# Earlier query weights on GpSimd, and two steps exchanged on VectorE, in a hybrid decoder step

## The chip, the cores and the metric

The kernel runs on one core of a Trainium2 chip. The metric is the device time in microseconds (us) of one execution; several executions are timed and the median is taken. The engines are TensorE (PE in the profile, with PEld for the loads of its weights), VectorE (DVE), ScalarE (ACT), GpSimd (POOL) and SyncE (SP, which here issues DMAs).

## The reference, cut to what matters

One inference step of one decoder layer on 560 tokens: 16 meta tokens and 512 prompt tokens as one sequence, and 8 running samples of 4 new tokens with states of their own. All data are 32-bit floats.

```python
def trunk(x, W, states):
    x = x + 0.5 * swiglu(rmsnorm(x, g_ff1), ...)     # 1024 -> 2816 -> 1024
    mix, new_st = mixer(rmsnorm(x, g_mix), W, l, st)
    x = x + mix
    x = x + 0.5 * swiglu(rmsnorm(x, g_ff2), ...)
    return rmsnorm(x, g_final), states

def mlstm_chunk(q, k, v, ig, logf, C0, n0, m0):      # 4 heads of 128, in the mixer
    b = jnp.cumsum(logf, axis=-1)
    D = jnp.where(causal, b[..., :, None] - b[..., None, :] + ig[..., None, :], -jnp.inf)
    inter = b + m0[..., None]
    m = jnp.maximum(jnp.max(D, axis=-1), inter)
    w_intra = jnp.exp(D - m[..., None])
    w_inter = jnp.exp(inter - m)
    s = jnp.einsum('bhtd,bhsd->bhts', q, k) * w_intra
    num = jnp.einsum('bhts,bhse->bhte', s, v) + w_inter[..., None] * jnp.einsum('bhed,bhtd->bhte', C0, q)
    den = jnp.sum(s, axis=-1) + w_inter * jnp.einsum('bhd,bhtd->bht', n0, q)
    h = num / jnp.maximum(jnp.abs(den), jnp.exp(-m))[..., None]
    ...                                               # w_state, decay from the last token
    C = decay[..., None, None] * C0 + jnp.einsum('bhs,bhse,bhsd->bhed', w_state, v, k)
    n = decay[..., None] * n0 + jnp.einsum('bhs,bhsd->bhd', w_state, k)
    return h, (C, n, m_last)
```

The mixer has 4 such heads beside 4 tiles of 128 channels of a gated linear recurrence (RG-LRU: a short convolution, two gates from small matrices, a scan over tokens). Both halves go through one output projection. The reference takes the prompt in chunks; the kernel takes all 528 prompt tokens at once, which is the same function. For the samples the state `C0` and `n0` of each sample enter, weighted by `w_inter`.

## The kernel before, in words

**Layout.** Tokens lie along the free dimension (560 columns; `TQ` = 544 without the 16 meta tokens), channels on the 128 partitions. Every matmul of large matrices is split: each factor is a rounded high part and a low rest (`whi`/`wlo`, `xh`/`xl`, `zh`/`zl`), and three products of parts are added. ACT makes the high part with a copy, DVE the low part with a subtraction.

**Stages.** The first feed-forward block, the mixer, the output projection, the second feed-forward block and the last norm follow one another. The change is in the mixer, which takes about 430 to 570 us of the span.

**Order.** In the mixer nothing is scheduled by a planner. `PLAN` is a table of step names; a loop calls them in that order under a manual schedule, so each engine gets its instructions in the order in which the steps issue them. A name is a step and a head or channel tile: `n1` is `do_n(1)`. Each engine works through its own list in order and waits by semaphores; SP issues the DMAs in the same order.

The steps that the change and the prediction touch:

- `v`, `k`, `q`, `x`, `y`, `o`: PE products of the input projection (L296), 8 row tiles of weights each, for one tile of 128 output channels; `ev`, `ek`, `eq`, `eo`: DVE takes the result out of the accumulator with the norm's factor (L991), giving `vT`, `kT`, `qT`, `og`.
- `L(h)`: DMAs of a head: `Ab`, `Eb` (stabilisers in a row, for all partitions), `Wb` (`w_inter` of the 32 sample tokens, for all partitions), `c0` (the states, 8 samples of 128 x 128; the profile calls it `c`).
- `am`: POOL adds the causal masks to `Ab`. `w`: ACT takes exponentials, giving the weights `W` (1376 columns: five key tiles against the queries they reach, the last 32 columns the samples). `s`: PE makes the scores `pA`, `pB`. `m`: DVE multiplies `W` by the scores (L1458).
- `sd`: POOL adds `W` over key tiles into `D` (L1464 to L1468), so that one sum over partitions is left for the denominator. `hd`: `D` is split into `zh` (ACT, L1320) and `zl` (DVE, L1321).
- `qw`: POOL makes the decayed queries of the samples: `qw` = q times `Wb`, `qn` = `qw` times n0, and then adds the samples' own weights to `qn`.
- `n`: PE's phase for numerator and denominator of a head: `state(b)` (L1489) is sample b's state matrix against its four columns of `qw`, `keys(i)` (L1493) is a tile of values against `W`, `den(i)` (L1497) sums `zh` and `zl` over partitions, L1508 is the samples' own values, L1512 the sum of `qn` over partitions.
- `cn`, `cm`, `f`, `cf`: the head's norm. ACT takes squares of `pn` into `sq` and `dd`; `cm` splits the squares (`sqh` by ACT, L1531; `sql` by DVE, L1532) and takes a maximum into `dd` (DVE, L1534); `f` sums them on PE into `pv` (L1541); `cf` adds `pv` to `dd` (DVE, L1548) and takes the root.
- `cw`, `p`, `cp`: the new state. POOL decays `c` (L1568), PE makes the outer products `px` (L1559), DVE adds them to `c` (L1582); then SP issues the DMA of `c` to `out_o_cs`, and POOL makes the new n (L1587, L1588).
- `a`, `b`: the two gates of a channel tile on PE (`prg`, L1191). `cd`: DVE's scan (L1243 to L1246). `ln`, `lr`: DVE sums the recurrence's squares (`lacc`, L1259), PE sums them over partitions (`pl`, L1265), ACT takes the root (`rl`, L1272), DVE refines it (L331).
- `tv`, `tk`: PE transposes v and k (L1354 to L1356) after POOL has copied the sample columns three times (`t`, L1351).

**Accumulators.** Products, gates, transposes, `pn`, `pv` and `px` all come from one ring of three PSUM tiles, and `pden`, `py` and a few others from a ring of two:

```python
psm = ctx.enter_context(tc.tile_pool(name="psm", bufs=3, space=PSUM))
psa = ctx.enter_context(tc.tile_pool(name="psa", bufs=2, space=PSUM))
def mm_tile(name="ps"):
    return psm.tile([P, 2, 512], F32, tag="mm", name=name)
```

A tile that PE wants to write must have been read by whoever took the third one before. `qw`, `qn`, `Wb` and `c0` have two buffers each; other intermediate rows come from a pool of 23.

Of the kernel before, what the change touches and what calls it, by code (L numbers as in the profile page):

```python
# [8 lines left out]
ALU = mybir.AluOpType  # L9
# [27 lines left out]
k0 gc  # L37
q0 ek0 gd
k1 eq0 gf ge L0 ex0 cx0 tv0 gp ek1 hq0 hk0 gq hx0 gh
x1 am0 hk1 ex1 cv0  # L40
q1 a0 eq1 w0 b0 ta0 s0 m0 cx1 tk0 tb0 ck0 ca0
v1 sd0 ev1 hq1 L1 hx1 cb0 hd0 qw0 vm0 n0 cw0 a1 cc0 sk0 b1 cd0 cn0 ta1 cm0 tb1
k2 ca1 cb1 ek2 ci1 tv1 am1
x2 f0 cv1 p0 ex2 cf0 tk1 ck1 cp0 cj1 cx2
q2 L2 s1 w1 m1 sd1 eq2 hx2 hq2
v2 ev2 cd1 hd1 a2 ta2 ca2 b2 cb2 vm1 sk1 qw1 tb2 n1 cw1 cc2 cn1 hk2 am2 ce0
x3 cm1 ex3 f1 cf1 ce1
k3 w2 cl1 tv2 cx3
q3 cv2 ek3 hx3 eq3 p1 s2 tk2 cp1 cd2 ck2
v3 qw2 m2 vm2 L3 a3 sd2 hd2 ev3 n2 cw2 ta3 ca3 b3 hk3 cb3 cn2 tv3 tb3 cc3 sk2 am3 cd3  # L50
o0 p2 hq3 cv3 ce2 ce3 eo0 cl2 cl3 cm2 w3 cp2
y0 qw3 to0 ln lr ey0 gy0
o1 eo1 mo0 s3 my0 m3 f2 sd3
y1 tk3 hd3 cf2 to1 ey1 gy1 ck3 so0 mo1 n3 cw3 sk3 cn3 cm3
y2 ey2 so1 f3
# [73 lines left out]
WO = (0, 512, 912, 1184, 1328, 1344)  # L129
# [10 lines left out]
def hymba_step(ctx, tc, xT, wgu1, wdn1, win, wout, wgu2, wdn2, consts, small, c0t, wrg,  # L140
# [610 lines left out]
    kv = spill.tile([LATER, 2, P, 516], F32, name="kv")  # L751
    kv4 = spill.tile([LATER, C16, 257], F32, name="kv4")
    mixer(tc, dict(locals()))


# [133 lines left out]
def mixer(ctx, tc, e):  # L889
    nc = tc.nc  # L890
    act, dve, pool, pe = nc.scalar, nc.vector, nc.gpsimd, nc.tensor
    C, X, sm, om, osm, one_m = e["C"], e["X"], e["sm"], e["om"], e["osm"], e["one_m"]
    nm, n2 = e["nm"], e["n2"]
# [7 lines left out]
    def slot(name="slot", dtype=F32):  # L901
        return mp.tile([P, 592], dtype, tag="s", name=name, bufs=SLOTS)
# [7 lines left out]
    def blk4(ap):  # L910
        return ap.rearrange("p (b j) -> p b j", j=4)
# [392 lines left out]
    D = [{} for _ in range(H)]  # L1304
# [155 lines left out]
    @step  # L1460
    def do_sd(h):
        W = D[h]["W"]
        S = D[h]["S"] = slot("D")
        pool.tensor_copy(S[:, 0:112], W[:, 0:112])  # L1464
        pool.tensor_tensor(S[:, 112:512], W[:, 112:512], W[:, 512:912], op=ALU.add)
        pool.tensor_tensor(S[:, 240:512], S[:, 240:512], W[:, 912:1184], op=ALU.add)
        pool.tensor_tensor(S[:, 368:512], S[:, 368:512], W[:, 1184:1328], op=ALU.add)
        pool.tensor_tensor(S[:16, 496:512], S[:16, 496:512], W[:16, 1328:1344], op=ALU.add)  # L1468

    @step  # L1470
    def do_qw(h):
        d = D[h]
        qw = d["qw"] = mp.tile([P, NB, 4], F32, tag="qw", name="qw", bufs=2)
        qn = d["qn"] = mp.tile([P, NB, 4], F32, tag="qn", name="qn", bufs=2)
        pool.tensor_tensor(qw, blk4(d["q"][:, 512:TQ]), d["Wb"], op=ALU.mult)
        n0 = d["n0"] = C[:, N0 + 8 * h:N0 + 8 * h + 8]
        pool.tensor_tensor(qn, qw, n0.unsqueeze(2).to_broadcast([P, NB, 4]), op=ALU.mult)
        qs = qn.rearrange("p b j -> p (b j)")[:32]
        pool.tensor_tensor(qs, qs, d["W"][:32, WO[5]:WO[5] + 32], op=ALU.add)

    @step
    def do_n(h):
        d = D[h]
        W, V = d["W"], d["V"]
        pn, pd = ps["n", h] = mm_tile("pn"), aux_tile("pden")

        def state(*bs):
            for b in bs:
                pe.matmul(pn[:, 1, 4 * b:4 * b + 4], d["c0"][:, b, :], d["qw"][:, b, :], start=b == 0, stop=False)  # L1489

        def keys(i):
            a = T0[i] - C16
            pe.matmul(pn[:, 0, a:512], V[:KROWS[i], i, :P], W[:KROWS[i], WO[i]:WO[i] + 512 - a],  # L1493
                      start=i == 0, stop=i == 4)

        def den(i):
            pe.matmul(pd, ones_r[1], d["Ss"][i], start=i == 0, stop=i == 1)  # L1497


        state(0, 1)  # L1500
        keys(0)
        state(2, 3)
        keys(1)
        state(4, 5)
        den(0)
        state(6, 7)
        keys(2)
        pe.matmul(pn[:, 1, 0:32], d["V5"], W[:32, WO[5]:WO[5] + 32], start=False, stop=True)  # L1508
        keys(3)
        den(1)  # L1510
        keys(4)
        pe.matmul(pn[:, 1, 64:96], one_m[1], d["qn"].rearrange("p b j -> p (b j)"), start=True, stop=True)  # L1512


# [211 lines left out]
```

## Time and profile before

| | |
|---|---|
| median of 3 runs | 1022.17 us (1020.84 to 1023.37) |
| profiled execution, its own time | 1023.64 us |
| its span, first to last instruction | 1021.9 us |
| mean granted TensorE clock | 0.993 |
| HBM read, written | 95.20 MB, 6.33 MB (99 GB/s over the span) |

Engines' busy shares, the chain that ended last, the waits and the rows around the change stand in the prediction. In such rows `L1489` is a line of the kernel as printed above, `out<-in` the program's names, and a bracket tells how long the engine had been idle and which instruction the profile puts down for its release. The granted clock is 1 where TensorE runs at full speed.

### The profile page before, as it was taken

The numbers are of one execution on the slowest core, as the hardware profiler recorded it, in microseconds if no ns is written. First come the engines' busy times: TensorE is split into PE (matmuls) and PEld (weight loads), VectorE is DVE, ScalarE is ACT, GpSimd is POOL, SyncE is SP. The second block draws the span as 40 slices with busy tenths as digits, with TensorE's granted clock in tenths as the row PEclk, the third lists the DMA queues.
The fourth block names the chain that finished last, engine by engine and source line by source line (L and its number), as shares of the span: only waits on it lengthen the run. The fifth ranks groups of instructions, "written<-read, shape, count | busy, mean of one in ns | idle before, by whom it ended". The sixth has DMA issues, their size and how long they took to land.

```text
span 1021.9 us, 20228 instructions
## 1 busy us (share of the span) xinstructions
PE 1013.1 (99%) x7778; PEld 997.5 (98%) x7778; DVE 832.3 (81%) x1480; ACT 559.5 (55%) x1074; POOL 127.3 (12%) x187
## 2 busy tenths in 40 slices
PE   9999999999999999999999999999999999999998
PEld 9999999999999999998999999999999999999997
DVE  7988888888788797889678765799888899859774
ACT  6544555565644464576666743554555665654543
POOL 1000000000000044382452202100000000000003
PEclk9999999999999999999799999999999999999999
DMA  6223233223332333325153133223323323335222
GB/s 234 92 79 103 89 100 104 94 95 103 89 104 68 106 116 130 102 81 146 35 133 103 57 104 108 73 64 103 112 87 102 105 94 114 93 102 156 81 70 96
DMA packets 61033, 102.85 MB, mean 101 GB/s; under 512 B 8560, under 2 KB 17024, under 8 KB 60936
## 3 DMA queue, kind: packets, MB, share of 16 engines
q1 hardware_dynamic: 60072, 101.11, 31.6%
q8 instruction: 61, 1.00, 0.4%
q10 hardware_dynamic: 864, 0.45, 0.2%
q14 instruction: 36, 0.29, 0.1%
HBM read 95.20 MB, written 6.33 MB: 99 GB/s over the span
## 4 chain that ended last, share of the span: by engine, by line
PE 88%; DVE 6%; ACT 2%; issue 1%; POOL 1%; DMA 1%; SPq 0%; DVEq 0%; POOLq 0%; ACTq 0%
PE pb L410 26%; PE pad L410 20%; PE pd L296 15%; PE po L296 7%; PE pu L296 4%; PE pg L296 3%; PE px L296 3%; PE pk L296 2%; PE py L296 1%; PE pq L296 1%; PE pn L1493 1%; DVE wlo L264 1%; PE pd L815 1%; PE pv L296 1%; PE pn L1489 1%
## 5 line engine op out<-in xcount | busy, mean ns | idle before, releaser
L259 ACT CAST whi<-raw 128x512 fp32r<-128x512 f32 (+2 forms) x289 | 172.3, 606 | 163.2 <-PE pad L410 41.3
L264 DVE TENSOR_TENSOR wlo<-raw,whi 128x512 fp32r<-128x512 f32 (+2 forms) x289 | 197.6, 700 | 65.5 <-ACT whi L259 62.7
L259 ACT CAST whi<-s 128x512 fp32r<-128x512 f32 x180 | 111.7, 621 | 105.2 <-PE pb L410 37.3
L264 DVE TENSOR_TENSOR wlo<-s,whi 128x512 fp32r<-128x512 f32 x180 | 124.1, 691 | 13.2 <-ACT whi L259 6.8
L410 PE MATMUL pad<-q21h,whi 128*128 128x280 f32 (+1 forms) x360 | 104.2, 290 | 0.1
L410 PE MATMUL pb<-qt4l,whi 128*128 128x280 f32 (+1 forms) x360 | 104.0, 289 | 0.0
L410 PE MATMUL pad<-q21l,whi 128*128 128x280 f32 (+1 forms) x360 | 104.0, 289 | 0.0
L410 PE MATMUL pad<-q21h,wlo 128*128 128x280 f32 (+1 forms) x360 | 104.0, 289 | 0.0
L410 PE MATMUL pb<-qt4h,whi 128*128 128x280 f32 (+1 forms) x360 | 103.9, 289 | 0.0
L410 PE MATMUL pb<-qt4h,wlo 128*128 128x280 f32 (+1 forms) x360 | 103.9, 289 | 0.0
L410 PEld LDWEIGHTS pad<-q21h,whi 128*128 128x128 f32 x360 | 67.8, 188 | 0.4 <-DVE z L429 0.4
L410 PEld LDWEIGHTS pb<-qt4h,whi 128*128 128x128 f32 x360 | 67.9, 189 | 0.0
L410 PEld LDWEIGHTS pb<-qt4h,wlo 128*128 128x128 f32 x360 | 67.8, 188 | 0.0
L410 PEld LDWEIGHTS pad<-q21l,whi 128*128 128x128 f32 x360 | 67.8, 188 | 0.0
L410 PEld LDWEIGHTS pb<-qt4l,whi 128*128 128x128 f32 x360 | 67.8, 188 | 0.0
L410 PEld LDWEIGHTS pad<-q21h,wlo 128*128 128x128 f32 x360 | 67.8, 188 | 0.0
L239 DVE TENSOR_TENSOR s<-raw 128x512 f32<-128x512 f32 x90 | 61.4, 682 | 2.0 <-DMA raw<-in_wdn 2.0
L296 PE MATMUL pd<-hl,whi 128*128 128x280 f32 (+1 forms) x294 | 61.6, 290 | 0.0
L296 PE MATMUL pd<-hh,whi 128*128 128x280 f32 (+1 forms) x294 | 61.4, 290 | 0.0
L296 PE MATMUL pd<-hh,wlo 128*128 128x280 f32 (+1 forms) x294 | 61.2, 289 | 0.0
L379 POOL TENSOR_TENSOR acc<-acc,sq 128x560 f32<-128x560 f32 (+1 forms) x6 | 9.1, 1518 | 405.3 <-ACT sq L378 405.3
L410 PE MATMUL pb<-q11h,whi 128*128 128x280 f32 (+1 forms) x180 | 52.4, 291 | 0.0
(470 smaller groups left out, 3008.0 us busy)
## 6 DMA issues: line engine op xcount, KB each, us to landing
raw<-in_wgu SPq DMA_DIRECT2D x174, 256.0 KB, 2.7
raw<-in_wdn SPq DMA_DIRECT2D x71, 256.0 KB, 2.7
raw<-in_win SPq DMA_DIRECT2D x50, 256.0 KB, 2.9
raw<-in_wout SPq DMA_DIRECT2D x16, 256.0 KB, 2.7
raw<-in_wdn SPq DMA_DIRECT2D x18, 192.0 KB, 2.4
c<-in_c0t SPq DMA_DIRECT2D x4, 512.0 KB, 5.4
out_o_cs<-c SPq DMA_DIRECT2D x4, 512.0 KB, 4.3
X<-in_xT SPq DMA_DIRECT2D x7, 280.0 KB, 5.4
```

What stands on the lines that cost most here:

```text
L239: dve.tensor_tensor(q[k], q[x], q[y], op=op)
L259: act.copy(ready[i][0][:, :src.shape[-1]], src)
L264: dve.tensor_tensor(lo, src, hi, op=ALU.subtract)
L296: state["mm"] = pe.matmul(ps[:, hf, :n], a[:, ws], b[k][:, c0 + hf * n:c0 + hf * n + n], start=first and j == 0 and i == 0, stop=last and ...
L379: (dve if d == KD - 1 else pool).tensor_tensor(self.acc[:, c0:], self.acc[:, c0:], s[:, c0:], op=ALU.add)
L410: pe.matmul(ps, a[:, k * P:k * P + P], b, start=first and k == 0 and i == 0, stop=k == KD // 2 - 1 and i == 2, skip_group_check=not first)
L815: pe.matmul(pd[d - TAIL][:, hf, :b - a], u[:, o:o + P], v[:, C16 + a:C16 + b], start=f == c0 and m == 0, stop=f == c1 - 1 and m == 2)
L1489: pe.matmul(pn[:, 1, 4 * b:4 * b + 4], d["c0"][:, b, :], d["qw"][:, b, :], start=b == 0, stop=False)
L1493: pe.matmul(pn[:, 0, a:512], V[:KROWS[i], i, :P], W[:KROWS[i], WO[i]:WO[i] + 512 - a], start=i == 0, stop=i == 4)
```

## The change

Five edits; no instruction is added or taken away, on any engine.

1. `qw` of each head stands right behind that head's masks (`am0 qw0`, `am1 qw1`, `am2 qw2`, `am3 qw3`). It stood behind `hd0` for head 0, behind `sk1` and just ahead of `n1` for head 1, ahead of `m2` for head 2, and at the head of row y0 for head 3.
2. The addition of the samples' own weights to `qn` moves from `do_qw` to the end of `do_sd`.
3. In row v2 `hd1` stands ahead of `cd1`: ACT's and DVE's split of head 1's `D` ahead of the scan of channel tile 1.
4. In row o0 `cp2` stands ahead of `cm2 w3`: the addition to head 2's state ahead of the split of its squares and of head 3's exponentials.
5. In `do_n` the second half of the matmuls has another order.

Two of the table's rows, and the code:

```diff
-v2 ev2 cd1 hd1 a2 ta2 ca2 b2 cb2 vm1 sk1 qw1 tb2 n1 cw1 cc2 cn1 hk2 am2 ce0
+v2 ev2 hd1 cd1 a2 ta2 ca2 b2 cb2 vm1 sk1 tb2 n1 cw1 cc2 cn1 hk2 am2 qw2 ce0
...
-o0 p2 hq3 cv3 ce2 ce3 eo0 cl2 cl3 cm2 w3 cp2
-y0 qw3 to0 ln lr ey0 gy0
+o0 p2 hq3 cv3 ce2 ce3 eo0 cl2 cl3 cp2 cm2 w3
+y0 to0 ln lr ey0 gy0
...
     def do_sd(h):
         ...
         pool.tensor_tensor(S[:16, 496:512], S[:16, 496:512], W[:16, 1328:1344], op=ALU.add)
+        qs = D[h]["qn"].rearrange("p b j -> p (b j)")[:32]
+        pool.tensor_tensor(qs, qs, W[:32, WO[5]:WO[5] + 32], op=ALU.add)
...
     def do_qw(h):
         ...
         pool.tensor_tensor(qn, qw, n0.unsqueeze(2).to_broadcast([P, NB, 4]), op=ALU.mult)
-        qs = qn.rearrange("p b j -> p (b j)")[:32]
-        pool.tensor_tensor(qs, qs, d["W"][:32, WO[5]:WO[5] + 32], op=ALU.add)
...
     def do_n(h):
         ...
         state(4, 5)
+        keys(2)
+        state(6, 7)
         den(0)
-        state(6, 7)
-        keys(2)
         pe.matmul(pn[:, 1, 0:32], d["V5"], W[:32, WO[5]:WO[5] + 32], start=False, stop=True)
         keys(3)
+        keys(4)
         den(1)
-        keys(4)
         pe.matmul(pn[:, 1, 64:96], one_m[1], d["qn"].rearrange("p b j -> p (b j)"), start=True, stop=True)
```

On POOL, around head 1's sum over keys (lines that begin with - stand there before, those with + after; `D` is the sum, `osm` the small outputs):

```order
 L1468 TENSOR_TENSOR D<-D,W 16x16
+L1470 TENSOR_TENSOR qn<-qn,W 32x32
 L1176 COPY osm<-xp 128x3
 L1177 COPY osm<-xp 128x24
-L1475 TENSOR_TENSOR qw<-qT,Wb 128x32
-L1477 TENSOR_TENSOR qn<-qw,C 128x32
-L1479 TENSOR_TENSOR qn<-qn,W 32x32
```

The three instructions leave the place behind the sum; the last of them now ends the sum, and the first two stand ahead of it, behind the masks.

On DVE, in row o0 and the start of y0 (`lacc` is the recurrence's sum of squares, `wlo` the split of the next weights):

```order
 L1259 TENSOR_TENSOR lacc<-lacc,lsq 128x544 x2
+L1582 TENSOR_TENSOR c_6287<-c_6287,px 128x1024
 L1532 TENSOR_TENSOR sql<-sq,sqh 128x544
 L1534 TENSOR_TENSOR dd<-dd,Eb 128x544
-L1582 TENSOR_TENSOR c_6283<-c_6283,px 128x1024
 L264 TENSOR_TENSOR wlo<-raw,whi 128x512 x2
 L331 SCALAR_TENSOR_TENSOR rlt<-pl,rl 128x544
```

The state addition moves up past `sql` and `dd`, and stands right behind `lacc`.

On PE, in head 0's phase `n`, which reads the same for the other heads:

```order
 L1489 MATMUL pn<-qw,c_5544 128x4 x2
+L1493 MATMUL pn<-W,V 128x272
+L1489 MATMUL pn<-qw,c_5544 128x4 x2
 L1497 MATMUL pden<-zh,ones_r_5096 128x512
-L1489 MATMUL pn<-qw,c_5544 128x4 x2
-L1493 MATMUL pn<-W,V 128x272
-L1508 MATMUL pn<-W,V_5687 128x32
+L1508 MATMUL pn<-W,V_5691 128x32
 L1493 MATMUL pn<-W,V 128x144
+L1493 MATMUL pn<-W,V 128x16
 L1497 MATMUL pden<-zl,ones_r_5096 128x512
-L1493 MATMUL pn<-W,V 128x16
```

Both `den` matmuls move back: the first past the last states and `keys(2)` (272 columns), the second past `keys(4)` (16 columns).

More of the change, by code (lines that the diff above doesn't have):

```diff
@@ L39 @@
 k1 eq0 gf ge L0 ex0 cx0 tv0 gp ek1 hq0 hk0 gq hx0 gh
-x1 am0 hk1 ex1 cv0
+x1 am0 qw0 hk1 ex1 cv0
 q1 a0 eq1 w0 b0 ta0 s0 m0 cx1 tk0 tb0 ck0 ca0
-v1 sd0 ev1 hq1 L1 hx1 cb0 hd0 qw0 vm0 n0 cw0 a1 cc0 sk0 b1 cd0 cn0 ta1 cm0 tb1
-k2 ca1 cb1 ek2 ci1 tv1 am1
+v1 sd0 ev1 hq1 L1 hx1 cb0 hd0 vm0 n0 cw0 a1 cc0 sk0 b1 cd0 cn0 ta1 cm0 tb1
+k2 ca1 cb1 ek2 ci1 tv1 am1 qw1
 x2 f0 cv1 p0 ex2 cf0 tk1 ck1 cp0 cj1 cx2
 q2 L2 s1 w1 m1 sd1 eq2 hx2 hq2
-v2 ev2 cd1 hd1 a2 ta2 ca2 b2 cb2 vm1 sk1 qw1 tb2 n1 cw1 cc2 cn1 hk2 am2 ce0
+v2 ev2 hd1 cd1 a2 ta2 ca2 b2 cb2 vm1 sk1 tb2 n1 cw1 cc2 cn1 hk2 am2 qw2 ce0
 x3 cm1 ex3 f1 cf1 ce1
@@ L49 @@
 q3 cv2 ek3 hx3 eq3 p1 s2 tk2 cp1 cd2 ck2
-v3 qw2 m2 vm2 L3 a3 sd2 hd2 ev3 n2 cw2 ta3 ca3 b3 hk3 cb3 cn2 tv3 tb3 cc3 sk2 am3 cd3
-o0 p2 hq3 cv3 ce2 ce3 eo0 cl2 cl3 cm2 w3 cp2
-y0 qw3 to0 ln lr ey0 gy0
+v3 m2 vm2 L3 a3 sd2 hd2 ev3 n2 cw2 ta3 ca3 b3 hk3 cb3 cn2 tv3 tb3 cc3 sk2 am3 qw3 cd3
+o0 p2 hq3 cv3 ce2 ce3 eo0 cl2 cl3 cp2 cm2 w3
+y0 to0 ln lr ey0 gy0
 o1 eo1 mo0 s3 my0 m3 f2 sd3
```

## The prediction

> **What bounds the kernel now.** I read the page's busy times first, then the chain that ended last, then the waits of PE by cost, then the timeline around each touched place, and last the granted clock in short windows.
>
> ```profile
> PE 1013.1 (99%) x7778; PEld 997.5 (98%) x7778; DVE 832.3 (81%) x1480; ACT 559.5 (55%) x1074; POOL 127.3 (12%) x187
> PE 88%; DVE 6%; ACT 2%; issue 1%; POOL 1%; DMA 1%; SPq 0%; DVEq 0%; POOLq 0%; ACTq 0%
> ...
> PE pn L1489 <- POOL qn L1477: 1.5, 1, 1.5
> PE warm L717 <- POOL ones L318: 1.1, 1, 1.1
> PE po L296 <- DVE c L1582: 0.9, 1, 0.9
> ```
>
> The reader is to see that PE works 1013.1 of the span's 1021.9 us. So what a new order can win is some idle time of PE, and whatever the granted clock does beside it. The waits' columns are who waits, for whom, sum in us, times, longest. Two of the three longest touch the change: head 1's `pn` (named as waiting for POOL) and output gate 1's `po` (for the state addition `c`). The `warm` wait is at the start, which the change leaves alone. I take the two places and then the smaller edits.
>
> **Head 1's pn: who really releases it.** Columns: start, duration, engine, line; in brackets the idle time before, and who is put down for it.
>
> ```profile
> 481.90 0.29 PE L1191 MATMUL prg<-xch,wrgl 128*128 128x292 f32 x1
> 482.44 0.62 ACT L1320 CAST zh<-D 128x512 fp32r<-128x512 f32 x1 [1.17 <-POOL D L1468]
> 482.88 0.73 DVE L991 TENSOR_TENSOR vT<-pv,r 128x560 f32<-128x560 f32 x1
> 483.11 0.24 POOL L1475 TENSOR_TENSOR qw<-qT,Wb 128x32 f32<-128x32 f32 x1
> 483.43 0.24 POOL L1477 TENSOR_TENSOR qn<-qw,C 128x32 f32<-128x32 f32 x1
> 483.68 0.52 PEld L1489 LDWEIGHTS pn<-qw,c 128*128 128x128 f32 x4 [1.72 <-POOL qn L1477]
> 483.71 0.58 PE L1489 MATMUL pn<-qw,c 128*128 128x4 f32 x4 [1.51 <-POOL qn L1477]
> ```
>
> PE stops at 482.19 (481.90 + 0.29) and goes on at 483.71. The trace names POOL's `qn` (L1477, ends 483.67). But the first matmul multiplies `qw` with `c`, and does not read `qn`: of POOL it needs L1475 alone, ended at 483.35. It also needs an accumulator: `pn` is the third matmul tile after row v2's `pv` (v2, a2, b2, n1) in a ring of three, so it gets the memory that `vT` (DVE L991) reads, and that ends at 483.61, 0.07 before the weight load starts. So I take `vT` for the releaser. The change issues `qw` and `qn` one stage earlier, which removes POOL's wait and leaves DVE's: `vT` stands ahead of everything that moves on DVE there. Gain: between 0 and 0.33 us (483.68 − 483.35, if `vT` does not count); I take 0. `hd1` ahead of `cd1` brings `zl` forward on DVE, behind `vT`; only `den(1)`, late in the phase, reads it. Gain 0.
>
> **The clock behind that stall.** Columns: window, its length, then busy time (and number) of PE, PEld, DVE, ACT, POOL, then granted clock, DMA share, GB/s.
>
> ```profile
> 484.00:485.00 1.00, 1.00 (x5) 0.73 (x5) 0.93 (x3) 1.00 (x2) 1.00 (x3) 0.81 0.92 309
> ...
> 497.00:498.00 1.00, 1.00 (x7) 1.00 (x5) 1.00 (x2) 0.34 (x1) 0.00 (x0) 0.50 0.00 0
> 498.00:499.00 1.00, 1.00 (x8) 1.00 (x8) 0.11 (x1) 0.16 (x1) 0.00 (x0) 0.86 0.23 47
> ```
>
> The granted clock halves inside the first window (0.81 = 1 − 0.38 × 0.5, so at 484.62) and is whole again at 498.28 (0.86 = 1 − 0.28 × 0.5): 13.66 us at half speed, right behind the stall. What that costs: head 1's phase against head 0's, up to the next product's first weight load, and the pitch of the products behind it.
>
> ```profile
> 443.39 0.54 PEld L1489 LDWEIGHTS pn<-qw,c 128*128 128x128 f32 x4
> 449.16 0.19 PEld L1191 LDWEIGHTS prg<-xch,wrgh 128*128 128x128 f32 x1
> 458.00 0.42 PE L296 MATMUL px<-xl,whi 128*128 128x280 f32 x2
> 458.26 0.42 PE L296 MATMUL px<-xh,wlo 128*128 128x280 f32 x2
> 493.58 0.55 PEld L296 LDWEIGHTS px<-xh,whi 128*128 128x128 f32 x2
> 494.26 0.67 PE L296 MATMUL px<-xl,whi 128*128 128x280 f32 x2
> 494.73 0.67 PE L296 MATMUL px<-xh,wlo 128*128 128x280 f32 x2
> ```
>
> Head 1 takes 493.58 − 483.68 = 9.90 us, head 0 takes 449.16 − 443.39 = 5.77: 4.13 lost. From 493.58 to 498.28, 4.7 us, pairs come every 0.47 instead of 0.26 us: 4.7 × (1 − 0.26/0.47) = 2.1 lost. Together 6.2 us, four times the stall itself. If the stall stays, so should this: I book 0, with both ends ±1.6 (a quarter of the period more or less).
>
> [...]
>
> **Output gate 1's po.** Row o0 now has `cp2` ahead of `cm2`: DVE adds `c` before it makes `sql` and `dd`.
>
> ```profile
> 544.21 1.54 DVE L1259 TENSOR_TENSOR lacc<-lacc,lsq 128x544 f32<-128x544 f32 x2
> 546.22 1.08 PE L1265 MATMUL pl<-lacc,ones 128*128 128x272 f32 x4
> 546.94 1.21 DVE L1582 TENSOR_TENSOR c<-c,px 128x1024 f32<-128x1024 f32 x1
> 548.21 0.53 PE L296 MATMUL po<-xh,whi 128*128 128x272 f32 x2 [0.91 <-DVE c L1582]
> ```
>
> Here too the wait is for an accumulator: `po` is the third tile after `px` of head 2, which `c` reads. After the change `c` starts behind `lacc`, at 545.75, and ends at 546.96; PE is busy with `pl` until 547.30. So PE starts `po` at 547.30, and the whole 0.91 us goes. `sql` and `dd` come 1.21 us later; `f2`, which reads `sql`, stands at the end of the next row of the table, many products later.
>
> **What is late next: head 3's pn.** PE arrives 0.91 us earlier at a phase whose inputs come from other engines:
>
> ```profile
> 549.10 0.71 ACT L1272 ACTIVATE rl<-pl,eps_c 128x544 f32<-128x544 f32 x1
> 549.84 0.72 DVE L331 SCALAR_TENSOR_TENSOR rlt<-pl,rl 128x544 f32<-128x544 f32 x1 [0.49 <-ACT rl L1272]
> ...
> 557.45 1.16 DVE L1458 TENSOR_TENSOR W<-pA,W 128x512 f32<-128x512 f32 x2
> 562.80 0.69 DVE L1321 TENSOR_TENSOR zl<-D,zh 128x512 fp32r<-128x512 f32 x1 [1.33 <-ACT zh L1320]
> 563.41 0.71 DVE L1548 TENSOR_TENSOR dd<-pv,dd 128x544 f32<-128x544 f32 x1
> 563.79 0.27 PE L1356 MATMUL pt<-ident,t 128*96 128x128 f32 x1
> 564.18 0.52 PEld L1489 LDWEIGHTS pn<-qw,c 128*128 128x128 f32 x4 [0.37 <-DVE dd L1548]
> ```
>
> DVE waits for ACT's `rl` (ends 549.81), and from there `rlt`, `W`, POOL's sum, ACT's `zh`, `zl` and `dd` follow one another; `dd` reads head 2's `pv`, whose accumulator `pn` takes. `rl` sits behind ACT's own work and a table load, not behind `po`. So `dd` ends at 564.12 as now, PE is there at 564.06 − 0.91 = 563.15, and the wait grows from 0.37 (by PEld) to 1.28: the 0.91 is given back. Bounds for the pair: −0.91 (all of that chain moves with PE) to 0; I take 0, since the chain's first link does not depend on `po`.
>
> **Order inside do_n.** No matmul comes or goes. Two loads of few rows wait for the matmul before them:
>
> ```profile
> 447.62 0.29 PEld L1508 LDWEIGHTS pn<-W,V 32*128 32x128 f32 x2 [0.36 <-issue]
> 448.21 0.48 PE L1497 MATMUL pden<-zl,ones_r 128*128 128x512 f32 x1
> 448.62 0.29 PEld L1493 LDWEIGHTS pn<-W,V 16*128 16x128 f32 x2 [0.25 <-issue]
> ```
>
> Before, the 32-row load stands behind `keys(2)` and the 16-row load behind `den(1)`, with 0.36 and 0.25 us of idle load time. Now they stand behind `den(0)` and `keys(3)`. What the other neighbours give no row shows; the bounds are both pauses gone (−0.6 a head) and one more of the larger kind (+0.36). I take +0.08, nearest to no change, since both small loads still follow a full-height one: +0.08 for heads 0 and 3, +0.12 for head 1 at half clock, nothing for head 2, whose delay shortens the wait ahead of head 3. Sum +0.3.
>
> **POOL.**
>
> ```profile
> L1475 POOL TENSOR_TENSOR qw<-qT,Wb 128x32 f32<-128x32 f32 x4 | 1.0, 246 | 0.0
> L1477 POOL TENSOR_TENSOR qn<-qw,C 128x32 f32<-128x32 f32 x4 | 1.5, 380 | 0.3
> L1479 POOL TENSOR_TENSOR qn<-qn,W 32x32 f32<-32x32 f32 x4 | 1.7, 427 | 0.3
> ```
>
> Twelve instructions, 4.2 us, all still there. `qw` and the first `qn` (0.63 a head) go behind the masks, where POOL next waits for DVE's `W`: 0. The third, 0.43, now ends the sum over keys; behind it queue `cw` and, for head 2, the copy of three transposed columns that PE's `tv3` reads. At most 0.43 of PE wait there, ahead of the slack at head 3: 0. The `out_o_cs` DMA of head 2 is issued 1.2 us earlier, the next `Wb` load under 1 us later behind POOL's `ns`; both have stages to spare.
>
> **Sum.** Stall 0, clock 0, `po` −0.91, head 3 +0.91, do_n +0.3, POOL 0: +0.3. The profiled execution took 1023.64, 1.47 above the median 1022.17, with which I go: 1022.5 us. A change under 0.3% (3.07 us) can't be told from none here.
>
> **Rivals.**
> B, faster: the half-clock period does not come. For it: the stall is one link, and what the clock does behind it is a matter of microseconds; the 0.91 us stall before `po` fell in full clock and was followed by none. Against: the stall and the sparse phase behind it stay as they are. Time: 1022.5 − 6.2 = 1016.3. Nor has any run shown, three of them lying within 2.5 us of one another, that the period comes in some executions only. Chance 0.14.
>
> [...]
>
> B2, faster: POOL was the releaser after all. The stall goes, too: −1.5 − 6.2, 1014.8. Against it stand the operands of L1489 and the 0.01 us between `qn`'s end and the load, too short beside the 0.07 behind `vT` or the 0.06 behind `c` at `po`. Chance 0.04.
>
> C, slower: the wait ahead of head 3's `pn` grows to 1.28 us, near the 1.51 that halved the clock at head 1, with the same sparse phase behind it. The price, by the one period seen: +6.2, 1028.7; a single quarter of it gives 1024.1, so it decides from two quarters on. Against: 0.91 did nothing at `po`, and the products ahead of `n3` are dense. Chance 0.12.
>
> D: the change does nothing at all to `po`, because something else than `c` holds it; same time within 1 us, part of the forecast.
>
> **Numbers.** Forecast 0.70, with its own range 1020.2 to 1024.8 (the runs' spread, 1.3 each way, and a quarter of the half-clock period). Faster 0.18 (B, B2), slower 0.12 (C). For 8 in 10 the range takes the forecast's own and most of B: 1015.6 to 1024.8.
>
> **What would show it.** Right: head 1's `pn` still starts within 0.1 us of `vT`'s end, now put down to DVE, and the clock is 0.50 for some 13 us behind it; `po` has no wait; the wait of head 3's `pn` is 1.1 to 1.4 us; from there to the end PE is as busy as now. Wrong: head 1 starting ahead of `vT`, no half clock there, or one behind head 3's `pn`.

## The result, and the profile after

| | before | after |
|---|---|---|
| median of 22 runs each | 1019.56 us | 1024.93 us |
| lowest to highest | 1018.32 to 1025.42 | 1023.34 to 1031.58 |
| profiled execution, time and span | 1023.64, 1021.9 | 1023.57, 1021.8 |
| its mean granted clock | 0.993 | 0.995 |

The ratio after/before is 1.0052, 95% interval 1.0035 to 1.0069: slower by half a per cent, 5.4 us between the medians. The forecast was 1022.5 us, no measurable change, in a range that ended at 1024.8. The median of before is 2.6 us lower than that of the three runs on which the forecast rested. It is a soft number: 11 of the 22 executions of before took under 1019.1 us and the other 11 from 1020.0 us on, and the median falls into the gap. Four executions of the later runs, at 1211 to 1395 us and a clock of 0.65 to 0.75, are left out of all counts and medians.

The two profiled executions differ by 0.07 us, so their comparison does not hold the loss. It does hold the forecast's small steps. First the waits of PE after (who, for whom: sum in us, times, longest), then the rows at head 1, at `po` and at head 3, then three windows of the clock:

```profile
PE pn L1489 <- DVE vT L991: 1.5, 1, 1.5
PE pn L1489 <- DVE dd L1548: 1.3, 1, 1.3
PE pt L1356 <- POOL t L1351: 1.1, 2, 0.8
```

```profile
482.68 0.73 DVE L991 TENSOR_TENSOR vT<-pv,r 128x560 f32<-128x560 f32 x1
483.46 0.39 PE L1489 MATMUL pn<-qw,c 128*128 128x4 f32 x2 [1.52 <-DVE vT L991]
...
544.38 1.22 DVE L1582 TENSOR_TENSOR c<-c,px 128x1024 f32<-128x1024 f32 x1
545.97 0.62 PE L296 MATMUL po<-xh,whi 128*128 128x272 f32 x2
...
563.48 0.72 DVE L1548 TENSOR_TENSOR dd<-pv,dd 128x544 f32<-128x544 f32 x1
564.25 0.50 PE L1489 MATMUL pn<-qw,c 128*128 128x4 f32 x3 [1.28 <-DVE dd L1548]
```

```profile
484.00:485.00 1.00, 1.00 (x5) 0.52 (x5) 0.93 (x4) 1.00 (x2) 1.00 (x1) 1.00 0.89 342
485.00:486.00 1.00, 1.00 (x6) 0.93 (x5) 1.00 (x1) 0.98 (x2) 1.00 (x2) 0.50 0.01 4
495.00:496.00 1.00, 1.00 (x9) 1.00 (x8) 0.58 (x1) 1.00 (x4) 1.00 (x5) 0.88 0.00 0
```

With POOL's `qw` a stage earlier, head 1's stall is as long as before (1.52 us) and now put down to `vT`. The wait of `po` is gone. Head 3's wait of PE is 1.28 us, where it was 0.12 (564.18 − 564.06; the 0.37 was the weight load's). The half-clock period lasts from 485.00 to 495.24, 10.24 us: three times 3.41, where it was four times in the trace of before. That one window of difference, some 1.6 us, was in the forecast's bounds; what it brought, 1.29 us by the time of `lacc` (shown below), is lost again by head 3, which starts at 564.25 against 564.18.

New is POOL's copy `t`: PE waits 0.77 us for it at `tv3` and 0.38 at `tk3`.

### The profile page after: what moved, and what is told of

The parts are those of the page before. It is cut to its first block, busy times and chain, and to the rows that moved or that the text cites. A ratio compares the mean times of both kernels' runs of the same rounds, so it can differ in the third digit from the quotient of the medians.

```text
span 1021.8 us, 20227 instructions
## 1 busy us (share of the span) xinstructions
PE 1011.1 (99%) x7778; PEld 996.8 (98%) x7778; DVE 833.8 (82%) x1480; ACT 559.6 (55%) x1074; POOL 127.7 (12%) x187
## 4 chain that ended last, share of the span: by engine, by line
PE 88%; DVE 6%; ACT 2%; issue 1%; DMA 1%; POOL 1%; SPq 0%; DVEq 0%; POOLq 0%; ACTq 0%
PE pb L410 26%; PE pad L410 20%; PE pd L296 15%; PE po L296 6%; PE pu L296 4%; PE pg L296 4%; PE px L296 3%; PE pk L296 2%; PE py L296 1%; PE pq L296 1%; DVE wlo L264 1%; PE pn L1493 1%; PE p L296 1%; PE pd L815 1%; PE pv L296 1%
## 5 line engine op out<-in xcount | busy, mean ns | idle before, releaser
L767 POOL TENSOR_TENSOR acc<-acc,sq 128x272 f32<-128x272 f32 (+2 forms) x10 | 9.6, 972 | 343.4 <-ACT sq L765 343.1
```

What stands on the lines that cost most here:

```text
L767: pool.tensor_tensor(acc[:, a:b], acc[:, a:b], s, op=ALU.add)
```

## The experiments

Every run lists the mean granted clock of its execution. 0.998 and more is called full clock here; 0.991 to 0.997 is taken for one half-clock period, as a rule of three or four windows of 3.41 us, 0.985 to 0.987 for two. The upper line is not sharp: one window alone at half clock would lower the mean by 0.0017 (an estimate: half of 3.41 in 1018 us), and the clock also falls behind the last matmul, which takes off up to 0.0013 in these traces (2.6 us at 0.50 at the end of the last run of "Taking head 1's stall away").

### The kernel before, again

> The kernel before, unchanged. Clock theory: the executions differ by how many 3.4 us clock windows run at half speed behind head 1's stall, about 1.6 us each; executions near 1018.5 then have a mean clock of 0.998 or more, those near 1022 about 0.995, those near 1023.6 about 0.993. Wait theory (the change's loss of 5 us is made of waits that it adds): the clock of the fastest and the slowest executions differs by less than 0.002, and the spread has another source.

Measured: 12 executions at 1021.7 to 1024.95 us, all between 0.992 and 0.994. But the kernel before ran beside it, too, as in every later comparison. Its executions there fall into two groups. In the four comparisons, 70 of 130 were at full clock, with medians of 1018.6 to 1018.8; the other 60 were at 0.992 to 0.994, mostly 1021.5 to 1024.1 us. So the clock theory holds. The trace on which the forecast rested (0.993) belongs to the second group, and by their times so do two of its three runs (1022.17 and 1023.37 us; their clock is not on record, and the third, 1020.84 us, lies between the groups). Which of the two an execution gets seems not to be drawn anew each time: 0 of 12 at full clock here, 17 of 34 beside them. The ratio of this kernel to itself came out at 1.0023, interval 1.0008 to 1.0038. Such intervals are too narrow here, a difference of 0.2% is not to be trusted, and shares of 12 executions say little when they are near one half.

The changed kernel had no execution at full clock: 0 of 22 in the first comparison, and 0 of 10 below.

### Each edit alone

Edits 1 and 2, the query weights (PLAN as in the change for `qw0` to `qw3`, and the addition moved to `do_sd`):

> Edits 1 and 2 alone (query weights one stage up, sample weights added at the end of the sum over keys). Clock theory: head 1's stall stays at about 1.5 us, now put down to vT; the wait before head 3's pn stays under 0.5 us; times as before, 1018.5 to 1024. Wait theory: the copies of the sample columns at tv3 and tk3 come 0.4 us later and PE waits for them, up to 1.1 us in all; 1 us slower than before.

Measured: median 1023.46 us, ratio 1.0016 (0.9996 to 1.0035). Head 1's stall stays at 1.50 us, `<-DVE vT`; head 3's wait is 0.16. 3 of 12 executions at full clock, median 1019.08, some 0.5 above before's full-clock executions (1018.61 in the same comparison). PE waits 0.8 us for `t` at `tv3`. Both theories had a part.

Edit 4:

```diff
-o0 p2 hq3 cv3 ce2 ce3 eo0 cl2 cl3 cm2 w3 cp2
+o0 p2 hq3 cv3 ce2 ce3 eo0 cl2 cl3 cp2 cm2 w3
```

> Edit 4 alone (addition to head 2's state ahead of the split of its squares). The wait of po (0.9 us) goes; ACT's table load ahead of yg now stands behind DVE's yg, 1.3 us, so head 3's pn starts no earlier and its wait grows to 1.2 to 1.4 us. Clock theory: that second long wait brings more half-clock windows in part of the executions; median 2 to 5 us above before. Wait theory: the two cancel, within 0.5 us of before.

Measured: 11 executions, median 1027.03 us, ratio 1.0049 (1.0025 to 1.0074). This edit alone has the whole loss. Its profiled execution took 1031.31 us at 0.986, with a half-clock period behind each of the two waits, 13.65 us behind the first and, by the mean clock, as much behind the second. The waits' ends in the timeline, and the windows in which the clock falls (granted clock 0.98 and 0.94):

```profile
483.85 0.58 PE L1489 MATMUL pn<-qw,c 128*128 128x4 f32 x4 [1.55 <-POOL qn L1477]
...
565.69 0.27 PE L1489 MATMUL pn<-qw,c 128*128 128x4 f32 x1 [1.49 <-DVE dd L1548]
```
```profile
484.00:485.00 1.00, 1.00 (x6) 0.75 (x7) 0.93 (x3) 1.00 (x2) 1.00 (x2) 0.98 0.96 358
566.00:567.00 1.00, 1.00 (x5) 0.62 (x5) 0.65 (x1) 0.98 (x2) 0.82 (x2) 0.94 0.00 0
```

Three of its executions took 1021.4 to 1021.8 us at 0.998, more than before's at that clock (1019.2 to 1020.2 over the four comparisons); no trace of such a one was taken, and where the 1 to 2 us lie stays open. One window at half clock would fit both the 0.998 and some 1.7 us (half of 3.41); that is an estimate and not shown.

Edit 5 (the order inside `do_n`):

> Edit 5 alone (order inside do_n). Clock theory, if the phase's density sets whether the clock halves: a median 2 to 5 us above before with more half-clock windows behind head 1. Wait theory: 0.1 us a head at most, the same as before within 0.5 us.

Measured: median 1018.49 us, ratio 0.9988 (0.9969 to 1.0008); 7 of 12 at full clock, median 1018.24, against 1018.61 for before. The density theory falls; the forecast's +0.3 us has the wrong sign, if anything. Edit 3 alone was not run.

### The changed kernel again, and without edit 4

> The changed kernel, unchanged. Clock theory: no execution at full clock throughout (none over 0.996), a half-clock period behind head 1, behind head 3, or behind both; those with both have a clock of 0.986 and take 1029 to 1032 us. Wait theory: full-clock executions exist and are 4 us slower than those of before.

Measured: 10 executions, median 1025.72 us, ratio 1.0057 (1.0037 to 1.0077), none over 0.995. The profiled one shows the other variant. The clock is full through head 1, although the stall there is 1.50 us, and falls behind head 3:

```profile
483.00:487.00 4.00, 3.18 (x17) 2.40 (x18) 3.93 (x7) 3.94 (x6) 3.18 (x5) 1.00 0.40 131
561.00:562.00 1.00, 1.00 (x2) 0.36 (x2) 0.94 (x2) 0.99 (x1) 1.00 (x2) 0.70 0.00 0
```
```profile
560.36 0.61 PE L1489 MATMUL pn<-qw,c 128*128 128x4 f32 x4 [1.28 <-DVE dd L1548]
```

> The changed kernel without edit 4 (cp2 back behind cm2 and w3). Theory that edit 4 brings the loss: the wait ahead of head 3's pn is under 0.6 us, full-clock executions (0.998 or more, 1018 to 1019.5 us) come back in a part of the runs, none is at 0.986. Rival, that the early query weights or the order of do_n make head 1 fall to half clock each time: no execution over 0.996, median 1023.5.

Measured: 8 of 12 at full clock, median of these 1018.26; the other four 1023.6 to 1024.5. Ratio 1.0004 (0.9983 to 1.0025), head 3's wait 0.15 us. Without edit 4 the other four edits leave the time as it was. The rival falls.

### Which stall halves the clock

The changes of the granted clock give the answer. In the seven traces with a half-clock period they lie whole numbers of 3.4133 us apart, within 0.02 us: in that of before the clock falls at 484.62 and again, behind the last matmul, at 1020.51, 157 such steps later. The record of the clock, in the traces of before and after, begins 477.87 us ahead of the first fall, 140 steps. So the borders of the windows can be counted back to each wait from the fall at the end, also in a trace that is at full clock until then:

```profile
1020.00:1021.00 1.00, 0.00 (x0) 0.00 (x0) 0.00 (x0) 0.00 (x0) 0.00 (x0) 0.76 0.27 64
```
```profile
1015.00:1016.00 1.00, 0.00 (x0) 0.00 (x0) 0.00 (x0) 0.00 (x0) 0.00 (x0) 0.97 0.00 0
```

The first row is of before (0.76, so at 1020.52), the second of the change without edit 4 (0.97, so at 1015.94). There head 1's stall begins at 482.12; 1015.94 − 482.12 is 156.39 windows, so it begins 2.07 us behind a border. In the table the position of each wait in its window, in us behind the border (an end below its start lies in the next window):

| trace | wait | begins | ends | clock halves |
|---|---|---|---|---|
| changed kernel | head 1 | 0.36 | 1.88 | yes |
| edit 4 alone | head 1 | 0.75 | 2.30 | yes |
| before | head 1 | 1.00 | 2.51 | yes |
| edits 1 and 2 | head 1 | 1.42 | 2.92 | yes |
| before, again | head 1 | 1.47 | 3.02 | yes |
| ACT copy added (below) | head 1 | 1.64 | 3.15 | no |
| without edit 4 | head 1 | 2.07 | 0.16 | no |
| edit 5 alone | head 1 | 2.19 | 0.33 | no |
| head 3 filled (below) | head 1 | 2.39 | 0.47 | no |
| changed kernel, again | head 1 | 2.84 | 0.93 | no |
| edit 4 alone | head 3 | 0.73 | 2.22 | yes |
| changed kernel, again | head 3 | 1.09 | 2.37 | yes |
| ACT copy added | head 3 | 2.25 | 3.33 | no |
| changed kernel | head 3 | 2.88 | 0.75 | no |

In these traces the clock halved, at the window's end, when a wait of 1.28 to 1.55 us lay in one window with the sparse phase behind it; it stayed when a border cut the wait, or when most of what else was in the window was the dense work ahead of it. All 14 waits (the one of 1.08 us among them) are on the right side of a start between 1.47 and 1.64. The rule was drawn from these waits; what speaks for it beyond them is the share it gives. Where the windows stand to a run's first instruction differs from execution to execution (counted back from the falls, the first border lies at 3.34 and 0.65 us in the two traces of before, at 0.31 and 1.61 in those of the changed kernel), and if all positions are equally frequent, head 1's wait halves the clock in 43 to 48% of before's executions (1.47 and 1.64 of 3.41, an estimate); 60 of 130 did, 46%.

In the windows of the seven waits that halved the clock PE was idle for 1.50 to 1.66 of 3.41 us (1.51 at head 1 before, 1.66 at head 3 with edit 4 alone), less than half of each.

Why the changed kernel never runs at full clock follows in part. At full clock its two waits begin 76.76 us apart (482.32 and 559.08 in the second trace): 22 windows and 1.67 us. An execution that escapes at head 1 (start 1.6 to 3.4) has head 3's start between about 3.2 and, over the border, 1.7, of which nearly all is the stretch that halves or close to it. Whether a position is left at which neither wait halves it, 14 waits cannot tell; 32 executions show none.

To test the cause directly I gave PE work during the waits:

```diff
 def do_n(h):
     ...
+        for _ in range(7 if h in (1, 3) else 0):
+            pe.matmul(pd, ones_r[1], d['ks'][0], start=True, stop=True)
         state(0, 1)
         keys(0)
```

> The changed kernel with seven matmuls more at the start of do_n for heads 1 and 3 (ones against a finished split, 512 columns, into pden, which den(0) overwrites): PE works through about 1.5 us of the two waits, and the waits end when they end. Theory that idle PE ahead of the two sparse phases is what halves the clock: all executions at 0.998 or more, 1017.5 to 1019 us, 5 us faster than the changed kernel. Rival, that the sparse phases themselves do it: half-clock periods as before, 1023 to 1032 us.

Measured: all 12 at full clock, 1019.0 to 1020.28 us, median 1019.56, 5.4 us faster than the changed kernel and 0.6 over the expected range. In the timeline the filling and head 1's first matmuls, 1.7 us later and with no wait; below, 20 us around them, with PE busy throughout at clock 1.00:

```profile
481.78 1.78 PE L1501 MATMUL pden<-zh,ones_r 128*128 128x512 f32 x7
483.46 0.39 PE L1489 MATMUL pn<-qw,c 128*128 128x4 f32 x2
```
```profile
480.00:500.00 20.00, 20.00 (x137) 18.11 (x136) 17.60 (x31) 14.78 (x24) 18.51 (x30) 1.00 0.21 68
```

Head 1's phase starts when it did (483.46), head 3's 0.2 us later, as the last of the seven matmuls ends behind `dd`; both are as sparse as they were, and only PE is not idle ahead of them. With `h in (3,)` in the same line:

> The same with the seven matmuls ahead of head 3 alone. Theory: only head 1 can halve the clock, as in the kernel before; a part of the executions is at full clock (1017.5 to 1019 us), the others at 0.993 to 0.995 (1022 to 1024), none at 0.992 or less. Rival (the loss has to do with head 1 alone): as the changed kernel, none at full clock.

Measured: 4 of 12 at full clock (1019.3 to 1019.7), eight at 0.993 to 0.997 (1021.1 to 1025.5), median 1022.55. As expected, full clock is possible again, and head 1 alone then decides, as it does before the change.

### Why head 3 is late: a table load behind a wait

DVE's `lacc` and ACT's rows ahead of `yg`, after the change. Before, the same load ran at 549.83, right behind `rl`.

```profile
542.92 1.54 DVE L1259 TENSOR_TENSOR lacc<-lacc,lsq 128x544 f32<-128x544 f32 x2
...
547.80 0.72 ACT L1272 ACTIVATE rl<-pl,eps_c 128x544 f32<-128x544 f32 x1
551.56 1.28 ACT L1283 ACT_TABLE_LOAD   x1 [3.04 <-DVE yg L991]
552.86 0.66 ACT L1283 ACTIVATE yg<-yg 128x544 f32<-128x544 f32 x1
```

`rl` is 1.30 us earlier than before (549.10), but that comes from ahead of edit 4, the shorter half-clock period above all: `lacc`, in front of the moved step, is 1.29 us earlier as well (544.21 before), and from `lacc` to `rl` it is 4.88 us here and 4.89 there. So times are best read from `lacc` on. ACT then waits for DVE's `yg` and only then loads its table. Head 2's `dd` starts 20.56 us behind `lacc` (563.48 − 542.92), before 19.20: 1.36 later, and head 3's `pn` with it (21.33 against 19.97). In the program as built, the activation that overwrites `yg` waits in the changed kernel for two things, DVE's `yg` and ACT's own `sqh` of head 2, whose input had the same memory; before, the second was already covered. With two waits, that for `sqh`, long done, stays on the activation, and that for `yg` stands as an instruction of its own ahead of the load. The trace of edit 4 alone has the load behind `yg`, too; that of the other four edits together has it right behind `rl`. One small copy takes the second wait away, because ACT then has waited for something later already:

```diff
 def do_lr(_):
     pl = ps["ln"][:, :, :272]
+    act.copy(seen[:32], D[3]["W"][:32, WO[5]:WO[5] + 1])
```

> The changed kernel with one small ACT copy ahead of rl (one column of W, 32 rows, into a scratch tile), which makes ACT's second wait of yg unneeded, so that the wait for DVE's yg stands on the activation and no longer on the table load. Theory that the table load behind DVE's yg makes head 3 late: that load runs while DVE is still at yg, dd ends 1.2 us earlier, the wait ahead of head 3's pn falls from 1.3 to 0.6 us or less, no execution at 0.986; up to 1 us faster than the changed kernel at the same clock. Rival, that the rest of the chain (POOL's sum, zh, zl) holds head 3: the wait stays at 1.2 us or more.

Measured: 5 of 12 at full clock again (median 1018.34), one at 0.987; median 1022.02, ratio 1.0007 (0.9984 to 1.0031). Its lines stand two lower.

```profile
544.34 0.71 ACT L1274 ACTIVATE rl<-pl,eps_c 128x544 f32<-128x544 f32 x1
545.07 1.28 ACT L1285 ACT_TABLE_LOAD   x1
548.06 0.66 ACT L1285 ACTIVATE yg<-yg 128x544 f32<-128x544 f32 x1 [1.70 <-DVE yg L992]
...
559.45 0.61 PE L1491 MATMUL pn<-qw,c 128*128 128x4 f32 x4 [1.08 <-DVE dd L1550]
```

From `rl` to `yg` it is 3.72 us, with the load behind the wait 5.06: 1.34 less. Head 3 starts 0.91 us earlier than in the second trace of the changed kernel, although `rl` is 0.44 later. The wait fell to 1.08 only, against the 0.6 that I expected, because PE comes 1.1 us earlier too: its waits for `og` (0.23 us) and for `t` at `tk3` (0.38) are gone with the late load. Behind `lacc`, at 539.39 here, head 3's `pn` starts after 20.06 us, against 19.97 before the change and 21.33 with the load behind the wait. In this trace the two waits begin 75.70 us apart, 22 windows and 0.61 us, and full clock is possible again.

### Taking head 1's stall away

```diff
-q2 L2 s1 w1 m1 sd1 eq2 hx2 hq2
-v2 ev2 cd1 hd1 ...
+q2 L2 s1 w1 m1 sd1 eq2 hx2
+v2 ev2 hq2 cd1 hd1 ...
```

> The kernel before with one step moved: hq2, the split of head 2's q, behind ev2, so that DVE makes vT 1.2 us earlier; nothing else changes. Theory that the 1.5 us stall ahead of head 1's pn is what halves the clock: the stall falls to 0.3 to 0.5 us, all executions have a clock of 0.998 or more, 1017 to 1018.5 us. Rival, that the sparse phase of head 1 halves the clock by itself: a part of the executions stays at 0.993 and takes 1021 to 1024 us.

A miss. Measured: six executions, median 1025.88 us, all at 0.991 to 0.993. `vT` came 1.3 us earlier, but the stall grew to 3.55 us, now for POOL's `qw`. It begins 2.05 us behind a border; the clock stays full at that window's end and falls at the next, 487.12, in whose window 2.18 us of the wait and the phase lie, as the rule above has it. POOL's sum over keys had slowed down beside DVE's new order. First POOL before, then here:

```profile
479.49 1.39 POOL L1466 TENSOR_TENSOR D<-D,W 128x272 f32<-128x272 f32 x1
480.95 0.83 POOL L1467 TENSOR_TENSOR D<-D,W 128x144 f32<-128x144 f32 x1
481.86 0.54 POOL L1468 TENSOR_TENSOR D<-D,W 16x16 f32<-16x16 f32 x1
```
```profile
479.66 2.60 POOL L1466 TENSOR_TENSOR D<-D,W 128x272 f32<-128x272 f32 x1
482.34 1.55 POOL L1467 TENSOR_TENSOR D<-D,W 128x144 f32<-128x144 f32 x1
483.98 1.37 POOL L1468 TENSOR_TENSOR D<-D,W 16x16 f32<-16x16 f32 x1
```

Edit 1 takes `qw` out of that line. So the same step on top of the changed kernel, without edit 4:

> The changed kernel without edit 4, and with hq2 behind ev2, as in the run of that edit alone, where POOL's qw then came 3.5 us late. Here qw is made a stage earlier, so only vT counts. Theory: the wait ahead of head 1's pn falls from 1.5 to 0.3 to 0.5 us, head 3's stays under 0.5, all executions at 0.998 or more, 1016.5 to 1018.5 us, faster than both kernels. Rival: POOL's slower sum over keys makes another input late (zh), the stall stays over 1 us and part of the executions is at 0.993.

Measured: all 12 at full clock, 1018.92 to 1020.11, median 1019.23; ratio 0.9990 (0.9977 to 1.0003). `pn` of head 1 starts at 481.97, PE's wait too short to be listed. The time is over the expected 1018.5: `f1` now waits 0.5 us for ACT's `sqh` and 0.9 for DVE's `sql`. With edit 4 and the small copy:

> The changed kernel with hq2 behind ev2 and with the small copy that frees ACT's table load. Theory: head 1's wait 0.3 to 0.5 us, head 3's about 1.1 us; half clock behind head 3 in a part of the executions only (1022 to 1024 us), the others at full clock, 1016.5 to 1018 us. Rival, that the 1.1 us wait is too short to halve the clock: all executions at full clock.

Measured: 11 of 12 at full clock (median 1019.37), one at 0.994 (1024.12); ratio 0.9992 (0.9977 to 1.0007). Head 3's wait of 1.10 us begins 1.36 us behind a border in the trace, and the clock stays full, where the longer waits that began at 1.42 and 1.47 halved it: the length counts too, and a wait of 1.1 us halved the clock in one of these 12 executions at most.

### What the edits cost at full clock

With the filling, executions differ little, and small terms can be read. All four ran in one comparison; before's own full-clock executions there had a median of 1018.79 us. `b_fill` is the kernel before with the filling for head 1.

> The kernel before with seven matmuls more at the start of do_n for head 1 (into pden, overwritten later). Theory that idle PE ahead of head 1 halves the clock: all executions at 0.998 or more, 1018.2 to 1019.2 us, faster than before in the median by what its half-clock executions cost, 1 to 4 us. Rival, that the fillers delay head 1's phase: 1019.5 us and more.

Measured: all 12 at full clock, median 1018.58; ratio 0.9978 (0.9965 to 0.9991).

> The kernel before with edit 5 (order inside do_n) and the filling for head 1. Theory that the order saves the loads' pauses: 0.3 to 0.6 us below the kernel before with the filling alone, 1017.6 to 1018.5 us, all at full clock. Rival, the forecast's term: 0.3 us above it.

Measured: 11 executions, 1018.35, all at full clock, 0.23 below `b_fill`, less than expected; ratio 0.9979 (0.9967 to 0.9991). In the traces it is 55.16 us from head 1's `pn` to `lacc`, in `b_fill` 55.52.

> The changed kernel without edit 4 and with the filling for head 1. Theory: all at full clock; the later copies at tv3 cost at most what the order inside do_n brings, 1017.6 to 1018.6 us, faster than both kernels. Rival: the copies' 0.8 us shows, 1018.8 us or more.

Measured: 1018.02, 1017.66 to 1018.50, all at full clock; ratio 0.9971 (0.9957 to 0.9985). The edits 1, 2, 3 and 5 with the filling are 0.56 below `b_fill`, and faster than the kernel before and the changed one.

> The changed kernel with the small copy that frees ACT's table load, and the filling for heads 1 and 3. Theory that the table load alone makes head 3 later than the forecast had it: 0.7 to 1.2 us below the changed kernel with the filling (which took 1019.0 to 1020.3), all at full clock. Rival: within 0.3 us of it.

Measured: 1018.53, all at full clock, 1.03 below the changed kernel with the filling (which ran in another comparison); ratio 0.9979 (0.9966 to 0.9992).

Five kernels had the filling ahead of each phase with a wait of over 1 us, and all their 59 executions were at full clock, against 70 of 130 of before; that is too many to be put down to a grouping of the executions.

The changed kernel with the filling lies 0.89 us above before's full-clock executions of its comparison (1019.56 against 1018.67), `b_fill` 0.21 below those of its own, `ld_fill` 0.26 below. So against `b_fill` the changed kernel is 1.1 us slower at full clock, and without the late table load 0.05 faster. The filling itself costs something at head 3, as its last matmul runs past `dd`: `pn` there starts 21.5 us behind `lacc`, without the filling 21.3, and with the small copy 20.4 against 20.1. Less these 0.2 and 0.4, an estimate, the change costs about 0.9 us at full clock: 1.3 for the table load, less 0.4 that the other terms bring.

## Why the prediction was wrong

- **Who releases head 1: right.** `vT`, 0.05 us before the matmul, and the stall as long as before.
- **`po`: right.** No wait, 0.91 us won.
- **Head 3: right in size, by luck.** The wait is 1.28 us as forecast, but out of other parts. "The chain's first link does not depend on `po`" held: `rl` stands 4.9 us behind `lacc` before and after. What failed is "`dd` ends ... as now": the chain had left out ACT's table load for `yg`, which edit 4 puts behind a wait, and `dd` came 1.36 us later by `lacc`. PE came later as well, so that the two made 1.28. With the load out of the way head 3's `pn` stands 0.09 us later than before the change and PE waits 1.08, near the 0.12 + 0.91 that the forecast's own mechanism gives: the 0.91 is given back, as it said. So the pair cost 1.36, where 0 was forecast and 0 was its upper bound.
- **`do_n`: wrong sign.** +0.3 forecast, −0.2 to −0.4 in two comparisons, near what they can tell, and −0.36 in the traces of the filled kernels.
- **POOL: too small.** "0" forecast, with 0.43 at most at `tv3`; PE waits 0.77 there, and 0.38 at `tk3`, which the forecast had not looked at and which is gone without the late table load. In the changed kernel the wait at `tv3` costs nothing that the traces show: from head 1's `pn` to `lacc` it is 55.17 us with edits 1, 2, 3 and 5 and the filling, 55.16 with edit 5 alone and the filling. In edits 1 and 2 alone that stretch is 61.07 us against 60.50 before, at half-clock periods of the same length, which fits the 0.5 us.
- **The clock: the step that failed.** "If the stall stays, so should this: I book 0." The period is not tied to the stall but to where the stall lies in a 3.41 us window (those of 1.28 to 1.55 us halved the clock with a start up to 1.47 us behind a border, not from 1.64 on). Before is at full clock in half of its executions, and the changed kernel in none. Rival C, half clock behind head 3, is what decides, at a chance of 0.12. As a second period on top of the first it came in 4 of 22 executions only (0.985 and 0.986); what the forecast missed is that C need not come on top: it also catches the executions that head 1 lets go. Its price of 6.2 us was near: the executions at 0.986 take 1031.5 us, 5.6 over those at 0.992 and 7.8 over those at 0.995. Rival B, no period, was what half of the executions of before already did; it was weighed as something that the change might bring, and its 1016.3 us is 2.4 below what they take (1018.7).
- **The range.** The two terms that it names, 1.3 and 1.6 us, add up to 2.9 each way, and it has 2.3. Neither term stands for what happened, so a wider range would have been luck as well. That the period varies by a quarter was an estimate then, which the one trace of before, with 13.66 us, could not show; the trace after has 10.24.

So of 5.4 us about 0.9 are lost at full clock, for which the table load is the reason; the other 4.5, by difference, are the half-clock periods that the longer wait at head 3 adds.

## What to carry to other kernels

Here a stall of 1.3 to 1.55 us ahead of a sparse phase cost the clock in some executions and not in others; a second such stall took away the executions that escaped, at 3 to 6 us each time, so count such stalls and not only their lengths. A trace of one execution tells by its clock row which of the groups it belongs to; ask for the clock of several executions before a sum is made against one. Where PE must wait, matmuls into a tile that is overwritten later kept the clock here (59 of 59 executions), and where two steps on DVE or ACT are exchanged, look where the waits ahead of table loads end up. Before two traces are compared by their times, look for a row ahead of the change by which to set them against each other: here their half-clock periods differed by a window.

## What the runs showed of the hardware

- In the seven traces with a half-clock period the granted clock changed on a grid of 3.4133 us. It fell to 0.50 behind each of the seven waits of 1.28 to 1.55 us that began 0.36 to 1.47 us behind a border and so shared a window with the sparse phase; once down it stayed for three or four windows (10.24 us after, 13.65 before), although PE was never idle in them (busy 10.25 of 10.25 and 13.65 of 13.65 us).
- POOL's additions took up to 2.5 times as long (0.54 and 1.37 us for 16x16) with another order of instructions on DVE at the same time. In the second order the 16x16 addition ends at 485.35 and DVE's scan beside it (L1246) at 485.34. What slows the additions no run took apart.
- The activation of `yg`, with two waits in the changed kernel, loads its table behind one of them (at 551.56, after 3.04 us of idle time; before at 549.83, right behind `rl`): 1.28 us that had been hidden.
